# Offsets of weight units inside their SBUF places, by kind of product

## The chip, the cores and the metric

The kernel runs on one core of a Trainium2 chip. The metric is the device time of one execution in microseconds; the median of several runs is compared. Five engines work side by side: TensorE (PE) multiplies, and loads the stationary operand of a product with an instruction of its own (PEld) that overlaps the product before it; VectorE (DVE), ScalarE (ACT) and GpSimd (POOL) do elementwise work; SyncE (SP) issues most transfers.

## The reference

Two decoder layers over 1024 tokens of width 1024. Each layer forms a modulated RMS norm of its input, one wide projection, three mixers on parts of its columns (sliding-window attention, retention, gated linear attention), a gate on each, an output projection, and a gated residual:

```python
h = rms_norm(x, pre_gain) * (1.0 + scale) + shift
proj = h @ w_in                      # 1024 x 3088
(aq, ak, av, ag, rq, rk, rv, rg, gq, gk, gv, gg, ga) = jnp.split(proj, IN_SPLITS, axis=-1)
...
y = jnp.concatenate([a_out, r_out, g_out], axis=-1) @ w_out
return x + gate * rms_norm(y, post_gain)
```

All of it is float32.

## The kernel before

**Products.** A float32 product is made of three products of a reduced float32 type: each operand is split into a high and a low part, and high x high, low x high and high x low are summed in PSUM (`PASSES`, `accum`). A projection of one 128-token tile by 256 columns is thus 3 x 8 = 24 matmuls. The weights of 256 columns are called a unit. There are four kinds of products with a unit:

- **plain** (`project`): the hidden state of one tile is the stationary operand, 128 columns; the unit is the moving one, 256 columns (272 for `gg`, which carries the 16 columns of the decay gate's low rank). Units `rg`, `rq`, `rk`, `rv`, `gv`, `kv` and `gg`.
- **turned** (`project_T`): 128 columns of the unit are stationary, the hidden state of two pairs of tiles is moving, 512 columns. Units `gqk`, `aq0`, `aq1`, `ag0`, `ag1`.
- **out** (`y_half`, and `y_last` with 256 columns): in layer 0 a tile of the mixers' output, named `mx`, is stationary and two `o` units are moving.
- **block** (`prod`): layer 1's output uses a scheme with seven products of half-size weight blocks (`W00`, `T1` and so on). A block is moving, 512 columns; an `mx`, `ma` or `a22` tile is stationary. T4 of the last tile is done in halves of 256 columns.

**Places.** Units, hidden states and blocks live in seven places of two large tiles, arena0 (places 0 to 2) and arena1 (places 3 to 6); `PLACES` has tile, offset and row width of each, in elements of 4 bytes, and `place(i)` gives a place as [high or low, k, columns]. `PLACE` says which place a unit takes in each layer, `TOK` which places the four pairs of hidden states take, `SW` the blocks. A row (one k) of an ordinary place has 256 elements, 1024 bytes, so every row begins at the same address modulo 512. Places 0 and 2 are wide, for `gg`: a row has 288 elements, 1152 bytes, so successive rows begin 128 bytes later modulo 512. In layer 0 the units `gg`, `rk`, `gv`, `aq1`, `ag1` are in place 0 and one pair of hidden states, and later `o1`, in place 2; in layer 1 those five units are in place 2, and one pair in place 0. A block has rows of 512 elements, 2048 bytes.

**Addresses.** SBUF is filled pool by pool: constants, arena0, the work tiles, then arena1. arena0 begins at byte 19,456 of a partition, 38 x 512. The work pool follows it and begins with 11 small tiles of 64 bytes, so its larger tiles (`t1`, the tiles for `kT` and `ma`, `mx`, `t2`, the staging tiles with `a22`) begin at 192 modulo 512. arena1 begins, after a pad of `APAD` = 32 bytes, at 153,600, 300 x 512. `GPAD`, a pad at the head of the work pool, is 0. The constant identity is at 128 modulo 512. In all that follows the distance is that of the moving operand's start less the stationary's, modulo 512: 0 for plain and turned products (0, 128, 256, 384 in turn where one of the two is in a wide place), 320 for out and block products.

**Order.** TensorE's instructions run in an order written out by the program: `mult` and `transp` add to a clock, and `pump` puts in the steps of smaller jobs whose due time has come (decays, attention, retention, norms). That order does not depend on addresses. Weights come by `load`: a transfer into a staging tile, the split into high and low on ScalarE, VectorE and GpSimd (L154, L542, L550), a flag for the products that wait.

Of the kernel before, what the change touches and what calls it, by code (L numbers as in the profile page):

```python
# [23 lines left out]
KT = D // P  # L24
# [16 lines left out]

LOG_CLAMP = -24.0

SLOT = KT * 512
WIDE = KT * 576
PLACES = {0: (0, 0, 288), 1: (0, WIDE, 256), 2: (0, WIDE + SLOT, 288)}
PLACES.update({3 + i: (1, i * SLOT, 256) for i in range(4)})
PLAIN = 2
SW = dict(W00=6, T1=3, W11=4, W10=5, T2=2, T3=0, T4=1)
TOK = ((1, 2, 3, 4), (3, 4, 0, 1))  # L50
PLACE = []
# [40 lines left out]
def trunk(ctx: ExitStack, tc: tile.TileContext, ins, cst, out):  # L92
# [3 lines left out]
    def skew(pool, name, n):  # L96
        if n:
            pool.tile([P, n // 4], F32, name=name, tag=name, bufs=1)
# [39 lines left out]

    arenas = [bp.tile([P, 2 * WIDE + SLOT], F32R, name="arena0")]

    def place(i):
        n, o, w = PLACES[i]
        return arenas[n][:, o:o + 2 * KT * w].rearrange("p (a k n) -> p a k n", a=2, k=KT)

    def both(x, y):
# [324 lines left out]


    def unit(l, name):
        return place(PLACE[l][name])


    queue, flying = [], []
# [35 lines left out]
    def used(l, name):  # L512
        await_flag(("w", l, name))
        return unit(l, name)

    def load(l, name, first=None):
        if l >= DEPTH:
            return
        c0 = COLS[name]
        src = w_out[l] if name[0] == "o" else w_in[l]  # L520
        wt = unit(l, name)
        sv = src.rearrange("(k p) n -> p k n", p=P)

# [35 lines left out]


    def sw(name):
        n, o, _ = PLACES[SW[name]]
        return arenas[n][:, o:o + KT * 512].rearrange("p (a k n) -> p a k n", a=2, k=4)

    def sw_load(k, i, j):
# [5 lines left out]
    def sw_split(name, k, st, key):  # L571
        w = sw(name)
        copy("sh" + key, w[:, 0, k], st)
        eng("sl" + key).tensor_tensor(w[:, 1, k], st, f(w[:, 0, k]), ALU.subtract)
# [8 lines left out]
    def sw_first(name):  # L583
        def conv(k, x, y=None):
            if y is not None:
                sw_diff(x, 0, k, x, y)
            if name[0] == "W" and name[1] == "1" and k > 1:
                w, g = sw(name), gnc[:, DEPTH - 1:DEPTH]
                A.activation(w[:, 0, k], x, AF.Copy, scale=g)
                V.scalar_tensor_tensor(w[:, 1, k], x, g, f(w[:, 0, k]), ALU.mult, ALU.subtract)  # L590
            else:
                sw_split(name, k, x, f"w{k}")
            if k == 3:
                flag(("sw", name))

        for k in range(4):
            if name == "T1":
                request(DEPTH - 1, 2, lambda k=k: (sw_load(k, 0, 1), sw_load(k, 0, 0)), lambda *s, k=k: conv(k, *s))
            else:
                i, j = int(name[1]), int(name[2])  # L600
                request(DEPTH - 1, 1, lambda k=k: (sw_load(k, i, j),), lambda *s, k=k: conv(k, *s))
# [62 lines left out]
    def pre(l, t, xt, early=False, soon=False):  # L664

        p, tt = divmod(t, 2)
        if tt == 0:
            hT[(l, p)] = place(TOK[l][p])
# [94 lines left out]
    skew(ap, "apad", APAD)  # L763
    arenas.append(ap.tile([P, 4 * SLOT], F32R, name="arena1"))
    with tc.issue_after(mark[0].ins), tc.issue_after(mark[3].ins):
# [497 lines left out]
    def prod(dst, a, name, start=True, stop=True, c=slice(0, 512)):  # L1263

        w = sw(name)
        await_flag(("sw", name))
        q = 0
        for i, j in PASSES:
            for k in range(4):
                mult(dst, a[:, i, k, :], w[:, j, k, c], start and q == 0, stop and q == 11)  # L1270
                q += 1
        pump()
# [411 lines left out]
B2, B1, BS, BST, MMB, SMB = 10, 8, 11, 5, 3, 3  # L1684
EN = {"shw0": "V", "shw1": "A", "shw2": "A", "shw3": "A", "slw0": "V", "slw1": "G", "slw2": "V", "slw3": "G", "sht2": "A", "sht3": "A", "sht4": "A", "slt2": "V", "slt3": "G", "slt4": "G", "sd": "V", "mh0": "A", "mh1": "A", "mh2": "A", "mh3": "A", "mf": "A", "ms0": "V", "ms1": "V", "ms2": "V", "ms3": "V", "yg0": "V", "yg1": "V", "ml0": "V", "ml1": "V", "ml2": "V", "ml3": "V", "mod0": "A", "mod1": "V", "qst": "S", "smh": "S", "sml": "S", "sm0": "S", "sm1": "S", "lao": "S", "sao": "S", "lmix": "S", "ssg": "S", "lsg": "S", "ssr": "S", "lsr": "S", "lx": "S", "sx": "A", "lw": "S", "lwm": "S", "whi0": "V", "whi1": "A", "whi2": "A", "whi3": "A", "wlo0": "V", "wlo1": "V", "wlo2": "V", "wlo3": "G", "xn0": "V", "xn1": "V", "hlo0": "V", "hlo1": "V", "rot0": "V", "rot1": "V", "rdec": "V", "kslo": "V", "qslo": "V", "vlo": "G", "kT": "A", "qT": "A", "sprev": "A", "pn": "G", "pf0": "A", "aoc": "A", "hng": "V", "mh": "A", "gso": "V", "mg": "V", "mgl": "V", "rT": "A", "rv": "A", "gv": "A", "gk": "A", "ak0": "V", "ak1": "V", "ak2": "V", "ak3": "V", "kd0": "G", "kd1": "G", "kd2": "G", "kx1": "G", "kx2": "G", "kx3": "V", "kx4": "V", "qb": "G", "stx": "V"}
L = {"sw1": 0.4, "ld1": 1.2, "ld2": 1.2, "ld1@1": 1.2, "ld2@1": 1.27, "swW00": 0.0, "swT1": 0.0, "swW11": 0.4, "swW10": 0.5, "tt1": 8.0, "tt2": 1.75, "tb1": 24.5, "tb2": 0.75, "pf3": 13.2, "pf1": 6.35, "pf2": 4.16, "mod1": 4.6, "mod2": 4.0, "mod3": 13.29, "mod4": 7.04, "mod5": 3.36, "mod6": 9.04, "pre1": 7.44, "kv1": 3.1, "kv2": 2.11, "aq1": 6.0, "aq7": 6.0, "ag1": 5.44, "aq2": 2.4, "aq6": 5.2, "aq3": 10.21, "aq4": 7.36, "aq5": 3.6, "hn1": 8.93, "hn2": 2.85, "gz1": 11.18, "gz2": 8.13, "gl1": 2.76, "gd3": 15.9, "gc1": 0.62, "gc2": 1.94, "gc3": 1.33, "gc4": 0.87, "gc6": 0.86, "gc5": 1.14, "rc1": 0.8, "rc2": 1.09, "rc3": 5.87, "rc4": 2.51, "fin1": 7.28, "lay1": 1.13, "gc4@1": 0.93, "mod2@1": 4.0, "mod3@1": 15.1, "mod5@1": 3.36, "mod6@1": 4.11, "pre1@1": 7.44, "kv1@1": 2.79, "kv2@1": 5.28, "aq1@1": 4.8, "aq7@1": 5.28, "ag1@1": 6.25, "aq2@1": 0.82, "aq6@1": 6.0, "aq3@1": 10.9, "aq4@1": 4.4, "aq5@1": 5.15, "hn1@1": 8.12, "hn2@1": 2.85, "gz1@1": 15.91, "gz2@1": 10.94, "gl1@1": 4.6, "gd3@1": 15.9, "gc1@1": 0.48, "gc2@1": 1.94, "gc3@1": 1.33, "gc6@1": 0.86, "gc5@1": 1.04, "rc1@1": 0.37, "rc2@1": 0.84, "rc3@1": 1.9, "rc4@1": 2.79, "fin1@1": 4.28, "lay1@1": 1.7}
CPAD, GPAD, APAD = 0, 0, 32
CHUNK = 7
LAG = 2
VDB = 8  # L1690
# [32 lines left out]
```

## Time and profile before

| | |
|---|---|
| median of 3 runs | 1008.04 us (1007.93 to 1008.37) |
| the profiled execution | 1009.94 us |
| its span, first to last instruction | 1008.2 us |
| TensorE busy | 971.4 us, 7133 products |
| weight loads busy | 829.8 us |
| VectorE, ScalarE, GpSimd busy | 689.2, 411.5, 233.5 us |
| mean granted TensorE clock | 0.984 |

The page and the trace's other views come from that one profiled execution. A busy share is the part of the span in which an engine works on something; products are pipelined and overlap their neighbours, so the time that one product really takes in a run is read from the spacing of starts, not from its mean duration. The chain of work that ended last is followed back from the last instruction to what released it, and so on; time on it is time that the end waits for. In a line such as `L170 PE MATMUL mm<-arena,mx 128*128 128x256 f32 x48 | 5.6, 276 | 0.0`, L170 is the line of the kernel (in the helper `mult`), mm is the PSUM tile written, arena and mx the tiles read, 128x256 the moving operand, x48 the count; then busy time in us, the mean of one in ns, and the idle time before. "mm<-arena,arena" are products with one operand in each arena tile, "mm<-arena" those with both in the same.

Between 40 and 320 us lie layer 0's projections with their mixers, from 320 to 530 its query and gate products, attention and output; 530 to 800 and 800 to 908 are the same for layer 1, and from 908 on its output in blocks.

### The profile page before, as it was taken

To read this page: it belongs to the slowest core of one execution; us is meant where nothing else is said; L and a number is where in the kernel's file an instruction comes from. 1 tells how busy PE (TensorE), PEld (TensorE's weight loads), DVE (VectorE), ACT (ScalarE), POOL (GpSimd) and SP (SyncE) were. 2 spreads that over 40 slices of the span, in tenths; PEclk is the share of its full clock that TensorE was granted. 3 is DMA by queue.
4 is the path that set the end of the run, shared out by engine and by line. 5 is a ranking of instruction groups with operands and counts; after the bars stand their busy time and mean duration, and the time that the engine had idled before them with its cause. 6 is when DMAs were issued, how large, how long until landed. Compare 5 with 4: busy or idle time off the path is not lost.

```text
span 1008.2 us, 19624 instructions
## 1 busy us (share of the span) xinstructions
PE 971.4 (96%) x7133; PEld 829.8 (82%) x7133; DVE 689.2 (68%) x1698; ACT 411.5 (41%) x1152; POOL 233.5 (23%) x275
## 2 busy tenths in 40 slices
PE   5798999999999999999999999999999999999996
PEld 1498999978998777777889999997899877777775
DVE  3779856847766688664488295685676577676876
ACT  2466421323332556643355242123333266563321
POOL 2210101232420234430113010113232033544100
PEclk8899999999999999999999999999999999999999
DMA  9832612423325245668646151343132433388884
GB/s 307 298 98 74 194 48 86 140 92 117 114 85 178 89 137 157 206 185 266 212 148 210 53 167 44 104 132 109 47 111 85 126 89 122 115 246 253 262 258 140
DMA packets 129969, 148.77 MB, mean 148 GB/s; under 512 B 14113, under 2 KB 94285, under 8 KB 129873
## 3 DMA queue, kind: packets, MB, share of 16 engines
q1 hardware_dynamic: 124176, 137.96, 44.8%
q10 hardware_dynamic: 5696, 9.56, 2.6%
q8 instruction: 56, 0.92, 0.4%
q14 instruction: 41, 0.33, 0.1%
HBM read 109.20 MB, written 36.18 MB: 144 GB/s over the span
## 4 chain that ended last, share of the span: by engine, by line
PE 76%; DVE 9%; DMA 5%; issue 4%; POOL 2%; ACT 2%; ACTq 0%; POOLq 0%; SPq 0%; DVEq 0%
PE mm L170 58%; PE aux L170 14%; PE aux L185 4%; DMA st<-in_w_in_dram 2%; POOL sm L645 2%; DMA xk<-in_x_dram 1%; DVE arena L542 1%; DMA a<-mixS 1%; DVE arena L718 1%; DMA st<-in_w_mod_dram 0%; DMA st<-in_w_out_dram 0%; DVE t L1257 0%; DVE t L335 0%; DVE t L676 0%; DVE t L710 0%
## 5 line engine op out<-in xcount | busy, mean ns | idle before, releaser
L170 PE MATMUL mm<-arena 128*128 128x256 f32 (+2 forms) x1824 | 300.2, 318 | 4.3 <-DVE t L1003 2.5
L170 PE MATMUL mm<-arena,arena 128*128 128x256 f32 (+2 forms) x1824 | 301.3, 319 | 1.8 <-DVE t L1003 1.8
L170 PEld LDWEIGHTS mm<-arena 128*128 128x128 f32 x1824 | 255.5, 191 | 28.9 <-issue 3.3
L170 PEld LDWEIGHTS mm<-arena,arena 128*128 128x128 f32 x1824 | 255.4, 191 | 26.3 <-issue 5.8
L645 POOL TENSOR_TENSOR sm<-sm,mhalf 128x1 f32<-128x1 f32 (+1 forms) x64 | 56.3, 880 | 350.4 <-DVE sm L644 335.2
L170 PE MATMUL mm<-arena,mx 128*128 128x512 f32 (+1 forms) x564 | 131.2, 389 | 2.1 <-ACT kept L1350 2.0
L170 PEld LDWEIGHTS mm<-arena,mx 128*128 128x128 f32 x564 | 102.4, 190 | 26.1 <-ACT kept L1350 2.4
L154 ACT ACTIVATE t<-aux 128x256 f32<-128x256 f32 (+2 forms) x124 | 55.9, 468 | 74.1 <-PE aux L185 61.8
L154 ACT ACTIVATE arena<-st 128x512 fp32r<-128x512 f32 x94 | 56.0, 626 | 53.1 <-PE mm L170 19.3
L542 POOL TENSOR_TENSOR arena<-st,arena 128x512 fp32r<-128x512 f32 x31 | 43.8, 1415 | 135.4 <-ACT arena L154 97.7
L940 POOL TENSOR_TENSOR smx<-smx,sm 128x512 f32<-128x512 f32 x32 | 35.7, 1117 | 127.2 <-DVE sm L939 119.8
L542 DVE TENSOR_TENSOR arena<-st,arena 128x512 fp32r<-128x512 f32 x77 | 59.5, 793 | 5.1 <-ACT arena L154 2.9
L936 ACT ACTIVATE smx<-smx,sm 128x129 f32<-128x129 f32 x128 | 49.9, 392 | 29.5 <-DVE sm L933 29.5
L185 PE MATMUL aux<-c_ident,t 128*128 128x128 f32 (+1 forms) x292 | 48.6, 284 | 7.9 <-DVE t L676 7.7
L372 DVE SCALAR_TENSOR_TENSOR acc<-st,c_act,acc 128x512 f32<-128x512 f32 x60 | 46.1, 768 | 13.0 <-DMA st<-in_w_mod_dram 12.5
L185 PEld LDWEIGHTS aux<-c_ident,t 128*128 128x128 f32 (+1 forms) x292 | 35.4, 145 | 14.9 <-DVE t L676 9.5
L170 PEld LDWEIGHTS aux<-t,mx 32*128 32x128 f32 (+1 forms) x896 | 39.5, 187 | 3.9 <-issue 2.2
L984 ACT ACTIVATE t<-aux 128x256 f32<-128x256 f32 x32 | 12.3, 384 | 73.6 <-PE aux L170 64.3
L708 ACT ACTIVATE t<-aux,mod,mod 128x128 f32<-128x128 f32 x68 | 25.8, 461 | 37.0 <-DVE t L1257 18.6
L170 PE MATMUL aux<-t,mx 32*128 32x32 f32 (+1 forms) x896 | 40.6, 272 | 0.0
L931 DVE COPY_PREDICATED smx<-c_curmask,aux 128x256 f32<-128x256 int32 x64 | 25.4, 445 | 18.3 <-ACT smx L154 14.8
L1257 DVE SCALAR_TENSOR_TENSOR t<-t,sm,t 128x512 f32<-128x512 f32 x32 | 24.0, 780 | 19.0 <-DMA t<-in_x_dram 11.2
(223 smaller groups left out, 1380.6 us busy)
## 6 DMA issues: line engine op xcount, KB each, us to landing
st<-in_w_in_dram SPq DMA_DIRECT2D x96, 256.0 KB, 3.1
st<-in_w_mod_dram SPq DMA_DIRECT2D x64, 256.0 KB, 2.8
st<-in_w_out_dram SPq DMA_DIRECT2D x52, 256.0 KB, 4.5
mx<-mixS SPq DMA_DIRECT2D x20, 512.0 KB, 5.1
mixS<-t SPq DMA_DIRECT2D x72, 128.0 KB, 3.6
wm<-in_w_mod_dram SPq DMA_DIRECT2D x12, 512.0 KB, 6.4
t<-in_x_dram SPq DMA_DIRECT2D x24, 256.0 KB, 4.4
t<-tabS SPq DMA_DIRECT2D x16, 256.0 KB, 4.1
```

The source lines that it names most:

```text
L154: A.activation(dst, src, AF.Copy)
L170: T.matmul(dst, lhsT, rhs, start=start, stop=stop)
L185: T.transpose(dst, src, idn)
L372: V.scalar_tensor_tensor(acc, wt, c_act[:, k:k + 1], acc, ALU.mult, ALU.add)
L542: e.tensor_tensor(lo, st, f(hi), ALU.subtract)
L645: G.tensor_tensor(r, r, mhalf[:, :w], ALU.pow)
L708: A.activation(hf[:, ks], at[kt], AF.Identity, scale=gain, bias=shift)
L931: V.copy_predicated(sv, curmask.unsqueeze(1).to_broadcast((P, 2, P)), pv[:, :, n // P - 1, :])
L936: A.activation(sm[:, h, :], sm[:, h, :], AF.Exp, bias=mx[:, h:h + 1], accum_out=sums[:, h:h + 1])
L940: eng("pn").tensor_tensor(sm[:, :, 0:128], sm[:, :, 0:128], rs.unsqueeze(2).to_broadcast((P, 4, P)), ALU.mult)
L984: A.activation(sq, po, AF.Square)
L1257: V.scalar_tensor_tensor(xt[j], yg[j], r, xt[j], ALU.mult, ALU.add)
```

## The change

The row width leaves `PLACES` and is given by whoever asks for a place: 256 elements for all but `gg`, which gets 320 (1280 bytes, so that its rows begin 0 and 256 bytes further modulo 512 in turn). No row of another unit or hidden state is 1152 bytes wide any more. Places grow by 128 elements, and a unit begins some elements into its place: 80 elements (320 bytes) for plain units and `gg`, 0 for turned and `o` units, 64 elements (256 bytes) for blocks. Hidden states begin at 0. `GPAD` becomes 320 bytes, which moves all work tiles by 320 (the larger ones then begin at 0 modulo 512), and `APAD` 224, so that with both pads arena1 is moved by 512 bytes and by the growth of arena0, which is a multiple of 512.

The distances after it are 320 for plain products (320 and 64 in turn for `gg`), 0 for turned, 0 for out and 256 for block products. What is computed, the number and order of TensorE's instructions and all transfers stay.

```diff
-SLOT = KT * 512
-WIDE = KT * 576
-PLACES = {0: (0, 0, 288), 1: (0, WIDE, 256), 2: (0, WIDE + SLOT, 288)}
-PLACES.update({3 + i: (1, i * SLOT, 256) for i in range(4)})
+SLOT = KT * 512 + 128
+WIDE = KT * 640 + 128
+PLACES = {0: (0, 0), 1: (0, WIDE), 2: (0, WIDE + SLOT)}
+PLACES.update({3 + i: (1, i * SLOT) for i in range(4)})
+TURNED = ("gqk", "aq0", "aq1", "ag0", "ag1")
+PLAIN_AT, TURNED_AT, OUT_AT, BLOCK_AT = 80, 0, 0, 64
...
-    def place(i):
-        n, o, w = PLACES[i]
+    def place(i, at=0, w=256):
+        n, o = PLACES[i]
+        o += at
         return arenas[n][:, o:o + 2 * KT * w].rearrange("p (a k n) -> p a k n", a=2, k=KT)
...
     def unit(l, name):
-        return place(PLACE[l][name])
+        at = OUT_AT if name[0] == "o" else TURNED_AT if name in TURNED else PLAIN_AT
+        return place(PLACE[l][name], at, 320 if name == "gg" else 256)
...
     def sw(name):
-        n, o, _ = PLACES[SW[name]]
+        n, o = PLACES[SW[name]]
+        o += BLOCK_AT
         return arenas[n][:, o:o + KT * 512].rearrange("p (a k n) -> p a k n", a=2, k=4)
...
-CPAD, GPAD, APAD = 0, 0, 32
+CPAD, GPAD, APAD = 0, 320, 224
```

## The prediction

> **What bounds the kernel now.** I read the busy shares first, then the chain of work that ended last, then that chain stage by stage, and last the spacing of single runs of products. All but the last two views are on the page or the answer about stages.
>
> ```profile
> span 1008.2 us, 19624 instructions
> PE 971.4 (96%) x7133; PEld 829.8 (82%) x7133; DVE 689.2 (68%) x1698; ACT 411.5 (41%) x1152; POOL 233.5 (23%) x275
> PE 76%; DVE 9%; DMA 5%; issue 4%; POOL 2%; ACT 2%; ACTq 0%; POOLq 0%; SPq 0%; DVEq 0%
> ```
>
> TensorE is busy for 96% of the span and makes up 76% of the chain. The other 24% are stretches in which it waits for a chain through VectorE, a transfer or GpSimd, and there a faster product gains nothing. The change touches only products of 128 rows that write a tile called mm (and a few that write aux), so I need their share of the path by stage. The first view has the busy time of all instructions that touch mm (its first PE number); the lines after it are the chain's shares in the same five stretches, in the same order.
>
> ```profile
> 40.00:320.00 280.00, 214.91 (x1480) 195.07 (x1481) 26.89 (x98) 18.41 (x56) 0.98 0.37 113
> 320.00:530.00 210.00, 171.25 (x699) 128.01 (x698) 24.21 (x36) 14.24 (x36) 1.00 0.56 176
> 530.00:800.00 270.00, 219.21 (x1562) 200.68 (x1561) 29.49 (x103) 20.15 (x62) 1.00 0.36 107
> 800.00:908.00 108.00, 76.01 (x297) 53.21 (x296) 11.86 (x18) 4.09 (x7) 1.00 0.47 142
> 908.00:1009.00 101.00, 68.95 (x296) 54.53 (x295) 13.14 (x20) 3.49 (x6) 0.96 0.71 226
> ...
> by line: PE mm L170 47.2%; PE aux L170 13.3%; issue 6.2%; PE aux L185 3.6%; POOL sm L645 3.0%; DMA st<-in_w_in_dram 2.7%; DVE arena L718 1.9%; DMA st<-in_w_mod_dram 1.8%; DVE arena L542 1.4%; DVE t L710 1.4%; DVE t L676 1.1%; DMA mixS<-t 1.
> by line: PE mm L170 78.8%; PE aux L170 15.3%; PE aux L185 6.0%
> by line: PE mm L170 61.9%; PE aux L170 13.4%; PE aux L185 4.0%; DMA st<-in_w_in_dram 3.5%; issue 3.0%; POOL sm L645 2.3%; DVE arena L542 1.5%; DVE t L1257 0.8%; DVE mx L1105 0.8%; POOL mx L802 0.7%; DVE t L990 0.6%; DVE t L1096 0.5%; DVE mx
> by line: PE mm L170 67.6%; PE aux L170 25.6%; PE aux L185 7.2%
> by line: PE mm L170 43.7%; DMA a<-mixS 7.8%; PE aux L170 6.4%; DMA st<-in_w_out_dram 4.9%; issue 4.3%; DMA t<-xs 3.2%; DVE t L1359 2.9%; DVE t L1354 2.8%; DVE t L1257 2.7%; POOL arena L574 2.7%; ACT st L1358 1.6%; DVE st L609 1.3%; DVE mx L
> ```
>
> Dividing path time by busy time gives the share of these products that counts: 0.472 x 280 / 214.9 = 0.61 in 40 to 320 us (layer 0's projections), 0.788 x 210 / 171.3 = 0.97 in 320 to 530 (its query and gate products and its output), 0.619 x 270 / 219.2 = 0.76 in 530 to 800 (layer 1's projections), 0.96 in 800 to 908 and 0.64 in the last stretch.
>
> How many products of each kind there are, from the groups kept apart by shape (name, shape, count, busy time, mean of one):
>
> ```profile
> L170 PE MATMUL mm<-arena,arena 128*128 128x256 f32 x1152 | 151.8, 286 | 0.0
> L170 PE MATMUL mm<-arena 128*128 128x256 f32 x1152 | 151.3, 286 | 2.5 <-DVE t L1003 2.5
> L170 PE MATMUL mm<-arena,mx 128*128 128x512 f32 x516 | 125.7, 400 | 2.1 <-ACT kept L1350 2.0
> L170 PE MATMUL mm<-arena,arena 128*128 128x512 f32 x480 | 123.3, 405 | 0.0
> L170 PE MATMUL mm<-arena 128*128 128x512 f32 x480 | 121.1, 400 | 0.0
> L170 PE MATMUL mm<-arena,mx 128*128 128x256 f32 x48 | 5.6, 276 | 0.0
> L170 PE MATMUL mm<-arena,a 128*128 128x256 f32 x24 | 3.0, 280 | 0.0
> ```
>
> So 2304 plain products of 256 columns, 960 turned ones of 512 columns; the gate unit gg adds 384 of 272 columns.
>
> **The change part by part.** No instruction is added, removed or put in another order; no transfer or wait is added. Only addresses move. What does the distance cost today? The timeline of TensorE has runs of one kind (start, length, count); the last three lines are pieces of the chain in order of time, in the same form. A run's spacing is the start of what follows less its own start, over its count, or its length less one mean duration, over count minus one.
>
> ```profile
> 530.46 5.84 PE L170 MATMUL mm<-arena,mx 128*128 128x512 f32 x49
> 536.14 7.91 PE L170 MATMUL mm<-arena,arena 128*128 128x272 f32 x62
> ...
> 586.16 5.92 PE L170 MATMUL mm<-arena 128*128 128x256 f32 x48
> 591.92 3.00 PE L170 MATMUL mm<-arena,arena 128*128 128x256 f32 x24
> 594.76 0.27 PE L185 MATMUL aux<-c_ident,ga 128*48 128x128 f32 x1
> ...
> 997.36 2.99 PE L170 MATMUL mm<-arena,a 128*128 128x256 f32 x24
> ...
> 334.71 2.66 PE L170 MATMUL mm<-arena 128*128 128x512 f32 x11
> ...
> 313.79 16.61 PE mm L170 x72
> 468.80 12.02 PE mm L170 x52
> 972.51 13.74 PE mm L170 x60
> ```
>
> Distance 0: the 48 products from 586.16 have weights and hidden state in plain 1,024-byte rows of arena 1, so moving minus stationary is 0 mod 512 throughout: (591.92 - 586.16) / 48 = 120.0 ns. With one operand in a wide place (1,152-byte rows; distance walks 0, 128, 256, 384), the 24 from 591.92 take (594.76 - 591.92) / 24 = 118.3 ns. Distance 320 is there already: layer 0's y_last multiplies o units, at 0, with an mx tile, at 192, and (192 + 320) is 512. Its run from 530.46 is one product of 512 columns, about 0.23 us by the rows below, and 48 of 256: (5.68 - 0.23) / 48 = 113.5 ns. The weight loads show it too:
>
> ```profile
> L170 PEld LDWEIGHTS mm<-arena 128*128 128x128 f32 x48 | 5.8, 192 | 0.0
> L170 PEld LDWEIGHTS mm<-arena,mx 128*128 128x128 f32 x47 | 5.4, 188 | 0.0
> ```
>
> One load takes 192 ns in the run at distance 0 and 188 ns in y_last's. That speaks for a meeting of the two reads. It isn't the whole story: the half-wide products of T4 at 997.36 are at 320 too, and take (2.99 - 0.28) / 23 = 117.8 ns. T4's rows are 2,048 bytes apart, y_last's moving rows 1,024 as the plain units' are, so y_last is the nearer row, and I take 113.5 with 117.8 as the other end.
>
> *Plain, 2304 products, to 320.* Of six plain units per layer two (rk, gv) lie in a wide place, and one of four hidden-state pairs does, so half the products (4/6 x 3/4) are at a constant 0 and save 6.5 ns; the others save 118.3 - 113.5 = 4.8. Mean 5.6, of which I count 93%, as the first one or two of 24 start after other work: 5.2 ns. 1152 in each projection stretch: 6.0 us of TensorE time each; on the path 0.61 x 6.0 + 0.76 x 6.0 = 8.2 us.
>
> *gg, 384 products.* Its run at 536.14 has (7.91 - 0.29) / 61 = 124.9 ns, with 0.29 for the last one's own duration. After, its 1,280-byte rows alternate between 320 and 64. No row shows 64; bounds are the present 125 and, with 256-column excess kept, 113.5 x 272/256 = 120.6. Midway, 2.3 ns: 0.9 us on TensorE, 0.6 on the path.
>
> *Turned, 960 products, to a clean 0.* The 72 at 313.79 (partly wide) have 16.61 / 72 = 230.7 ns. The 11 at 334.71 lie wholly in arena 1 at distance 0 and take (2.66 - 0.39) / 10 = 227.0. What is gained is that no unit or hidden state is strided any more: 3.7 ns, 87% of them in undisturbed runs, 3.1 us on TensorE, 2.8 on the path (most lies in the stretches with 0.96 and 0.97).
>
> *Layer 0's output, 360 products of 512 columns, from 320 to 0.* The 52 at 468.80 have 12.02 / 52 = 231.2 ns; at the turned run's 227.0, 4.2 ns, 1.5 us. y_last's 48 go from 113.5 to 120.0, plus 0.3 us of TensorE. There GpSimd's clearing of a gla tile is on the chain, not TensorE (a piece of the chain, quoted here), so it costs nothing; with that cover gone, 0.3.
>
> ```profile
> 530.92 1.82 POOL mx L802
> ```
>
> *Blocks of layer 1's output, some 330 products, from 320 to 256.* No run is at a constant 256. Now 13.74 / 60 = 229.0 ns. Bounds: 222.5 (the whole 6.5 ns between 120.0 and 113.5 gained) and 236 (the slowest spacing of a longer run: (337.75 - 331.14) / 28, quoted below). I take no change, as the rows at 320 and at a clean 0 lie only 2 ns apart; the ends are -1.4 and +1.5 us at 0.64.
>
> ```profile
> 331.14 6.68 PE L170 MATMUL mm<-arena 128*128 128x512 f32 x28
> 337.75 0.98 PE L170 MATMUL aux<-kT,mx 64*128 64x256 f32 x12
> ```
>
> *Side effects.* GPAD moves every work tile by 320. Products between two work tiles keep their distance. Transposes read the constant identity against a work tile, so theirs changes from 448 to 128. No row has 128; they hold about 4% of the chain (L185 in the lines above), 42 us, and if they spread by the same 6% as 113.5 to 120 do, that is 2.5 us either way; I take 0. Both arenas stay at a multiple of 512 (320 + 192 more bytes before arena 1).
>
> Sum: 8.2 + 0.6 + 2.8 + 1.5 = 13.1 us. VectorE, next with 9% of the chain, may be late in places where TensorE now ends it; I take 13. The profiled execution took 1009.94 us, 1.7 beyond its span and 1.9 above the median of 1008.04; it would be 997, and a median run **995.0 us**.
>
> The page "SBUF — State Buffer" of the Trainium skill, section "Who interferes with whom", speaks against all this: TensorE's two read ports (moving operand and weight load) are independent, and TensorE never waits on anyone in SBUF. By that rule addresses cost nothing and the sum would be 0. The trace of this case disagrees at 120.0 against 113.5 ns for one shape, but agrees in so far as 117.8 comes close to 118.3.
>
> **The rivals.**
> - *320 is worth little (T4's row).* y_last's 113.5 is then due to its stationary tile (rows of 512 bytes), and plain products settle near 117.8: 2.2 ns where they were at 0, 0.5 on the others, mean 1.35 x 0.93 x 2304 = 2.9 us, 2.0 on the path; with the other terms (0.6 of gg halved) 6.6: 1001.5 us. For it: 24 products at 320. Against it: 48 products, nearer in row step. 20%.
> - *Address is not the cause.* The spread comes from neighbours (other engines' traffic, entry into the run); the change does not do what it says: 1008 us. For it: one distance has both 113.5 and 117.8. (The page of the Trainium skill named above would make this the outcome.) Against it: the run of 48 at distance 0 holds 120.0 with a slower weight load throughout. 10%.
> - *Slower: 320 is the worse place for a full sweep.* The hidden state as stationary, in 1,024-byte rows, meets the moving read at 320 in the middle of each sweep, as 512-column products show it: 229.0 at 320 against 227.0 at 0. Plain products then cost 2 ns or more above 120; at 124, near gg's present spacing, +4.9 ns on 2304 x 0.69 = 7.8 us, less the 4.3 of turned and output: 1011.5 us, or 1013 with blocks at their upper end. It decides from about 121.6 ns for plain. 7%.
> - *Another engine becomes the bound.* In the stretches with 0.61 and 0.76 the weight conversions on VectorE and the transfers of w_in are already on the chain; if they are late wherever plain runs get short, two thirds of the 8.2 go: 1000.5 us. 9%.
>
> **How the numbers follow.** The forecast, 995.0, has 54%; its own range is 989 to 1000 (blocks -1.4 to +1.5, transposes 2.5 either way, gg, and up to 3 us hidden). With 20, 10, 7 and 9% for the rivals the range for 8 in 10 is 988 to 1004: it leaves out the no-change and slower cases. Faster by over 0.2% (about what a measurement tells from no change, 2 us): 54 + 20 + 9 = 83%; same 10%; slower 7%.
>
> **What would show it.** Right: plain runs of 48 near 113 to 114 ns with weight loads of 188 ns, runs of turned products with 227 and less spread, TensorE busy down by 15 to 18 us, the gain found in 40 to 320 and 530 to 800. Wrong: plain runs at 117 or above, blocks above 230, or TensorE's busy time down without the span following, with w_in transfers and VectorE growing on the chain.

## The result and the profile after

| | before | changed |
|---|---|---|
| median of 20 runs each, us | 1008.14 | 1004.82 |
| lowest and highest, us | 1004.78, 1011.52 | 1001.55, 1007.72 |
| profiled execution, us | 1009.94 | 1001.56 |

The ratio is 0.9962 (95% interval 0.995 to 0.9974): 3.8 us less, 2.6 to 5.0 (the medians differ by 3.3). The forecast was 995.0, with 988 to 1004 as range; the direction was right, the forecast gain more than three times too large. The two profiled executions differ by 8.4 us, more than twice what the medians say, as single runs of one kernel spread over 6 to 7 us. What the change did is therefore read from spacings.

The page of the changed kernel (span, busy shares, chain by engine):

```profile
span 999.8 us, 19626 instructions
PE 964.1 (96%) x7133; PEld 827.7 (83%) x7133; DVE 691.6 (69%) x1698; ACT 410.8 (41%) x1152; POOL 235.2 (24%) x275
PE 75%; DVE 10%; DMA 7%; issue 3%; ACT 3%; POOL 1%; SPq 0%; POOLq 0%; DVEq 0%; ACTq 0%
```

The bound is where it was: TensorE 96% busy and three quarters of the chain. Part of the 8.4 us lies even ahead of the products that were changed. The piece of the chain with the first four products that read the modulation's weights ends at 26.87 us in before and at 25.05 in the changed kernel: 1.8 us of the difference arise before any unit is used. In e6, the changed kernel executed again (below), the same piece ends at 26.59. That is run-to-run spread and no gain of the change.

Now the timeline of TensorE in the changed kernel, at the places that were shown of before (start, length, count):

```profile
523.20 6.37 PE L173 MATMUL mm<-arena,mx 128*128 128x512 f32 x50
529.41 8.02 PE L173 MATMUL mm<-arena,arena 128*128 128x272 f32 x62
...
579.12 5.82 PE L173 MATMUL mm<-arena 128*128 128x256 f32 x48
584.77 2.99 PE L173 MATMUL mm<-arena,arena 128*128 128x256 f32 x24
...
308.43 7.53 PE L173 MATMUL mm<-arena,arena 128*128 128x512 f32 x32
315.79 9.23 PE L173 MATMUL mm<-arena 128*128 128x512 f32 x40
324.95 0.77 PE L173 MATMUL aux<-kT,mx 64*128 64x128 f32 x10
...
964.10 5.60 PE L173 MATMUL mm<-arena,mx 128*128 128x512 f32 x24
969.54 2.88 PE L173 MATMUL mm<-arena,a 128*128 128x512 f32 x12
...
988.58 3.03 PE L173 MATMUL mm<-arena,a 128*128 128x256 f32 x24
```

Read as before. The 48 plain products at 579.12, now at distance 320, take (584.77 - 579.12) / 48 = 117.7 ns; before, at 0, it was 120.0. That is not y_last's 113.5 but the 117.8 of T4's halves. y_last itself, moved from 320 to 0, takes (529.41 - 523.20 - 2 x 0.23) / 48 = 119.8, where it had 113.5. T4's halves, moved from 320 to 256, take (3.03 - 0.28) / 23 = 119.6. gg takes (8.02 - 0.29) / 61 = 126.7, where it had 124.9: worse. The 72 turned products at 308.43 have (324.95 - 308.43) / 72 = 229.4, where they had 230.7, and the blocks from 964.10 on (969.54 - 964.10) / 24 = 226.7, where they had 229.0. The weight loads tell distances 320 and 0 apart (the plain run, then y_last; the second number behind the first bar is the mean duration in ns):

```profile
L173 PEld LDWEIGHTS mm<-arena 128*128 128x128 f32 x47 | 5.6, 188 | 0.0
...
L173 PEld LDWEIGHTS mm<-arena,mx 128*128 128x128 f32 x47 | 5.7, 192 | 0.0
```

The two kinds have changed roles: with 256 columns 192 ns belongs to distance 0, not to a kind of product. y_last shows one thing more. Its moving o units begin at 0 in both kernels; only mx, the stationary operand, was moved, and the spacing went from 113.5 to 119.8. So the moving operand's own address doesn't set the price by itself.

So that all kinds can be compared over all kernels, this table has the mean spacing from one product's start to the next one's, in ns, over all products of a kind, without those that were followed by other work or a wait (spacings of over 136, 143 and 243 ns for 256, 272 and 512 columns are left out, and with them most first products of a run after other work; 86 to 97% of a kind remain). It is worked out from the single records of each kernel's trace; the kernels' labels are explained below.

```
                     plain   gg     turned  output 512  blocks 512
before               118.9   124.6  231.2   231.3       229.0
changed              117.7   126.5  229.1   227.9       227.3
e2_plain0            119.7   125.5  229.2   227.9       227.5
e3_plain384          118.7   126.5  229.2   227.9       227.4
e5_plain32_gg448     117.1   123.9  229.1   227.9       227.3
e7_worst             119.7   125.4  234.0   234.2       234.2
e8_plain112          115.3   125.1  229.1   227.9       227.4
e9_plain192          115.8   123.5  229.1   227.9       227.4
e10_plain112_gg192   115.4   123.5  229.2   227.8       227.2
products, about      2160    340    830     344         320
```

The output's 231.3 before mixes two things. Half of these products read o1, which lay in a wide place: the 15 runs of 24 fall into eight at 232.3 to 233.3 ns and seven at 229.0 to 230.2, as many as there are with o1 and without. After, the same two groups have 227.7 and 228.0 on the mean. So by the move from 320 to 0 alone a product gains 1.5 ns, and by that and the end of the stride together 5.2; the prediction's "from 320 to 0" at 231.2 took the mixture for the distance.

### The profile page after: what moved, and what is told of

The parts are those of the page before. It is cut to its first block, busy times and chain, and to the rows that moved or that the text cites. A ratio compares the mean times of both kernels' runs of the same rounds, so it can differ in the third digit from the quotient of the medians.

```text
span 999.8 us, 19626 instructions
## 1 busy us (share of the span) xinstructions
PE 964.1 (96%) x7133; PEld 827.7 (83%) x7133; DVE 691.6 (69%) x1698; ACT 410.8 (41%) x1152; POOL 235.2 (24%) x275
## 4 chain that ended last, share of the span: by engine, by line
PE 75%; DVE 10%; DMA 7%; issue 3%; ACT 3%; POOL 1%; SPq 0%; POOLq 0%; DVEq 0%; ACTq 0%
PE mm L173 57%; PE aux L173 14%; PE aux L188 4%; DMA st<-in_w_in_dram 2%; POOL sm L650 1%; DMA st<-in_w_out_dram 1%; DVE arena L546 1%; DMA wm<-in_w_mod_dram 1%; DMA t<-mixF 1%; DMA xk<-in_x_dram 1%; DVE arena L723 1%; DMA mx<-mixS 1%; DVE t L715 1%; DMA st<-in_w_mod_dram 0%; DVE t L338 0%
## 5 line engine op out<-in xcount | busy, mean ns | idle before, releaser
L173 PE MATMUL mm<-arena,arena 128*128 128x256 f32 (+2 forms) x1824 | 297.7, 316 | 0.3 <-DVE t L1008 0.3
L173 PEld LDWEIGHTS mm<-arena,arena 128*128 128x128 f32 x1824 | 252.5, 188 | 23.7 <-issue 4.1
L173 PE MATMUL mm<-arena,mx 128*128 128x512 f32 (+1 forms) x564 | 128.3, 384 | 1.7 <-ACT kept L1355 1.7
```

The costliest lines, as they stand in the source:

```text
L173: T.matmul(dst, lhsT, rhs, start=start, stop=stop)
```

## The experiments

The theory after the result: the distance sets a few steady spacings, and 320 has two of them, 113.3 and 117.8. Rival A: y_last's 113.5 came from its stationary tile, whose rows are 512 bytes apart where a hidden state's are 1024. Rival B: the address is not the cause at all.

**e1_map: the price by itself.** A kernel with nothing but products. Each run of 24 has the three passes of `accum`; only the moving operand's offset changes.

```diff
+DIST = [int(d) for d in range(0, 512, 32)]
...
+                s0 = STAT + (a * KT + k) * sstep
+                m0 = MOV + d // 4 + (w * KT + k) * mstep
...
+    for d in DIST:
+        for m in (4, 2, 1):
+            turns(m)
+            run("wide", d)
+        for m in (4, 5, 6):
+            turns()
+            run("fill", 320, m, 512)
+            run("wide", d)
```

> Only products are run, on the input's values, and nothing of the layers is computed: per distance 0 to 480 in steps of 32 bytes, runs of 24 products of 256 columns (rows of 1024 bytes; six runs, entered from transposes or from products of 512 columns), of 256 columns with stationary rows of 512 bytes (two runs), of 272 columns with moving rows of 1280 bytes (two), of 512 columns in two halves (two). Theory 1 (the distance sets a small number of steady spacings, and 320 has two of them): at 320 most runs settle at 117.8 ns and a few at 113.3, whatever the stationary row; at 0 and 256 all at 120.0; near 116.7 at 384; 512 columns 226.7 at 0 and 256 and 229 at 320; 272 columns 126.7 at 320. Rival A (the stationary tile's rows of 512 bytes made the 113.5 of the kernel before): the runs with 512-byte stationary rows give 113.3 at 320 and those with 1024-byte rows 117.8. Rival B (address is not the cause): one spacing at all distances.

Mean spacing of a run's last products, ns; where the runs of a distance differ, the lowest and highest. Distances from 256 on repeat the value 256 below to 0.1 ns (wide at 160 and 416: 118.6 and 118.5 highest), so one period is given.

```
distance                  0/256  32/288  64/320  96/352  128/384      160/416      192/448      224/480
256, rows of 1024 (6x)    120.0  116.7   117.8   120.0   118.4-120.0  117.1-118.6  113.3-117.8  118.1-118.5
256, stat. rows 512 (2x)  120.0  116.7   117.8   120.0   118.2-120.0  117.2-118.6  113.3-117.8  118.3-118.5
272, rows of 1280 (2x)    125.6  125.8   126.7   125.4-  126.7        123.3-123.8  123.3        125.4-126.7
                                                 126.7
512 in two halves (2x)    226.7  233.3   228.9   233.3   232.9        234.3        233.3        233.3
```

Three runs of 256 columns in the timeline, at distances 0, 320 and 448, each seen through a window that leaves out a run's beginning (the row's start is that of its first product in the window):

```profile
39.32 2.08 PE L57 MATMUL wide<-arena 128*128 128x256 f32 x16
...
530.15 2.16 PE L57 MATMUL wide<-arena 128*128 128x256 f32 x17
...
722.81 1.86 PE L57 MATMUL wide<-arena 128*128 128x256 f32 x15
```

(2.08 - 0.28) / 15 = 120.0 ns, (2.16 - 0.28) / 16 = 117.5 and (1.86 - 0.28) / 14 = 112.9, each to some 0.7 by the rows' rounding. The core ran nothing else, so rival B falls. Rival A falls too: stationary rows of 512 and of 1024 bytes give the same spacings. e1 moves the moving operand alone; that the stationary one counts as much is shown by y_last above and by e7 below, whose turned units, stationary, are moved to distance 160 and take 234.0 where the map has 234.3. The theory holds, with two corrections: the period is 256 bytes, not 512, so 320 is the same place as 64, and in this quiet kernel 320 gave 117.8 in eight runs of eight; the two states appeared at 192 and 448 (113.3 once, 117.8 five times, at equal distances and with only the run ahead of them differing). At 384 the 116.7 that was expected did not come.

**e2_plain0 and e3_plain384: plain units elsewhere in the changed kernel.**

```diff
-PLAIN_AT, TURNED_AT, OUT_AT, BLOCK_AT = 80, 0, 0, 64
+PLAIN_AT, TURNED_AT, OUT_AT, BLOCK_AT = 0, 0, 0, 64
```

That is e2; e3 has 96 elements for plain.

> The changed kernel with plain units and gg at 0 instead of 320 bytes, all else as changed: what is left is the gain of turned, output and block products and of the unstrided rows. Theory 1: plain runs at 120.0 ns, 2.2 ns above the changed kernel, about 2300 x 0.93 x 2.2 = 4.7 us more TensorE time, two thirds of it on the path, so 3 us slower than the changed kernel and within 1.5 us of before (ratio to before 0.998 to 1.001). Rival B: the same time as the changed kernel (0.996).

> The changed kernel with plain units and gg at 384 bytes instead of 320. Theory 1, with the rows of the kernel before at a constant 384 (116.7 ns for 256 columns, 123.3 for 272): plain runs 1.1 ns and gg 3.4 ns below the changed kernel, 2.4 + 1.2 us of TensorE time, two thirds on the path: 2.4 us faster than the changed kernel, ratio to before about 0.994. Rival B: the same time as the changed kernel.

e2: 0.9988 of before (0.9968 to 1.0008), median 1007.58. Plain runs of 119.7 ns in the table, 2.0 above the changed kernel's. The ratio lies in the 0.998 to 1.001 expected, 2.6 us above the changed kernel's 0.9962, where the table gives (2.0 x 2160 - 1.0 x 340) x 0.69 = 2.7 (0.69 is the prediction's path share of plain products, the mean of 0.61 and 0.76). The two intervals overlap (the changed kernel's is 0.995 to 0.9974), so the times alone hardly tell them apart; the spacings do. It isn't the plain units' share in the gain over before either, as 119.7 is itself dearer than before's 118.9. Whether turned and output alone gain anything isn't shown by the time, only by their spacings. e3: 0.9977 (0.996 to 0.9994), and not the 0.994 expected. Plain takes 118.7 ns and gg 126.5, as the map has them at 384. The 116.7 of before "at a constant 384" had been read where unit and hidden state both lie in wide places. Both begin at 0 there and their rows step together, so the distance is 0 throughout and not 384; e4 gives 116.7 for such rows at 0.

**e4_finer: steps of 8 bytes, and rows that step.** The same kernel with `range(0, 256, 8)`, and runs whose moving rows (or both operands' rows) are 1088 or 1152 bytes apart.

> Again products alone, nothing of the layers: distances 0 to 248 in steps of 8 bytes (the first map repeats after 256), 256 columns entered in three ways, 272 columns (rows of 1280 bytes), 512 columns; and at every 32 bytes 256 columns whose moving rows, or both operands' rows, step by 1088 or 1152 bytes. Theory 1: the spacings move between 113 and 120 ns (256 columns) and 226 and 235 (512) in steps of 64 bytes or less, the two-state places lie around 192, and none lies steadily below 116.7. Rival (a line of 32 bytes or more is what counts): the eight distances within 32 bytes give the same spacing.

```
256 columns, three entries each, ns (the middle one where they differ by less than 0.6)
distance   0      8      16           24     32           40     48     56     64     104    112          120
spacing    120.0  120.0  113.3-118.7  120.2  116.7-117.8  120.0  118.3  120.0  117.8  120.0  113.3-114.8  122.2
distance   128          136          144          168    176    184    192    200          208    232    248
spacing    118.4-120.0  120.4-121.2  118.2-119.1  122.3  119.3  120.0  113.3  120.0-122.2  118.9  123.0  121.3
512 columns: 226.7 at 0, 246.7 at 104, 238.8 at 72, 240.0 at 88 and 168, 228.8 at 64; the other distances 231 to 240
both operands' rows 1152 bytes apart: 116.7 at seven of eight distances, 120.0 at 224; both 1088: 117.3 to 120.0
moving rows alone 1088 or 1152 bytes apart: 116.7 to 118.8
```

These are means over a run's last twelve products. Eight bytes decide: 112 has 113.3 (114.8 from one entry, which comes to 113.4 in its last eight) between 120.0 at 104 and 122.2 at 120. The rival, that all distances within 32 bytes cost the same, falls, and so does my "none lies steadily below 116.7": 112 and, here, 192 do. No odd multiple of 8 is below 119.7.

**e5_plain32_gg448 and e6_after_again.**

```diff
-PLAIN_AT, TURNED_AT, OUT_AT, BLOCK_AT = 80, 0, 0, 64
+PLAIN_AT, TURNED_AT, OUT_AT, BLOCK_AT = 8, 0, 0, 64
+GATE_AT = 112
...
-        return place(PLACE[l][name], at, 320 if name == "gg" else 256)
+        at, w = (GATE_AT, 320) if name == "gg" else (at, 256)
+        return place(PLACE[l][name], at, w)
```

> The changed kernel with plain units at 32 bytes (116.7 ns in the first map) and gg at 448 (rows then at 448 and 192, 123.3 ns). Theory 1: plain runs 1.1 ns and gg 3.4 ns below the changed kernel, 2.4 + 1.2 us of TensorE time, two thirds on the path: 2.4 us faster than the changed kernel, ratio to before 0.994. Rival (the path no longer takes gains in the projection stretches): the same as the changed kernel.

> The changed kernel beside the others on one chip: ratio to before 0.995 to 0.9975, by all theories.

e5: 0.9957 (0.9938 to 0.9976), median 1003.47; the changed kernel beside it: 0.997 (0.9948 to 0.9991), median 1004.75. Plain is at 117.1 and gg at 123.9, so the map carries over, but 1.3 us between the medians, where 2.4 were expected and the table gives (0.6 x 2160 + 2.6 x 340) x 0.69 = 1.5, lies within the intervals: the time decides neither for the theory nor for the rival.

**e7_worst: the dear distances.**

```diff
-PLAIN_AT, TURNED_AT, OUT_AT, BLOCK_AT = 80, 0, 0, 64
+PLAIN_AT, TURNED_AT, OUT_AT, BLOCK_AT = 0, 24, 40, 40
```

> The changed kernel with plain units and gg at 0 (distance 0, 120.0 ns), turned units at 96 bytes (distance 160, 234.3), o units and blocks at 160 bytes (distance 160, 234.3). Theory 1, by the first map: turned 7.6 ns x 830 x 0.93 = 5.9 us, output 2.5, blocks 1.6, plain 3.3: 13 us slower than the changed kernel, ratio to before about 1.009. If the address is not the cause, or the path hides it: within 3 us of the changed kernel.

1.0061 (1.0039 to 1.0084), median 1014.11: 0.0099 above the changed kernel's ratio, 10 us where 13 were expected (9.4 by the medians against e6, which ran beside it). Distances alone make 1% between two kernels. The 13 took the map's steady spacings (234.3 against 226.7). By the table the kinds differ by 4.9 ns (turned), 6.3 (output), 6.9 (blocks) and 2.0 (plain), gg gaining 1.1; with the counts in its last line and the path shares of the prediction (0.93, 0.97, 0.64, 0.69, 0.69) that is 3.8 + 2.1 + 1.4 + 3.0 - 0.3 = 10.0 us. The path shares thus agree with the time, within its interval of some 3 us; what was off is that turned products at the beginning of a run aren't at the steady spacing (229.1 on the mean, 226.7 at the end).

**e8_plain112, e9_plain192, e10_plain112_gg192: the state that the forecast had counted on.**

```diff
-PLAIN_AT, TURNED_AT, OUT_AT, BLOCK_AT = 80, 0, 0, 64
+PLAIN_AT, TURNED_AT, OUT_AT, BLOCK_AT = 28, 0, 0, 64
```

That is e8; e9 has 48 elements for plain, and e10 has 28 and, as e5, a `GATE_AT`, here of 48.

> The changed kernel with plain units and gg at 112 bytes. In the finer map 256 columns took 113.3 to 114.8 ns there from all three entries, and 272 columns 123.3. Theory 1, and with it the forecast's own sum at a price of 113.5: plain runs 4.4 ns and gg 3.3 ns below the changed kernel, 2160 x 4.4 = 9.5 and 1.1 us of TensorE time, two thirds on the path: 7 us faster than the changed kernel, about 0.990 of before. Rival (a quiet map doesn't carry over; with the layers' other work the runs fall into the slower state): plain at 117 to 120, within 2 us of the changed kernel.

> The changed kernel with plain units and gg at 192 bytes. The two maps had 113.3 ns in four of nine runs there and 117.8 in five; 272 columns 123.3. Theory 1: between the changed kernel and the one at 112 bytes, 1 to 6 us faster than the changed kernel, with plain runs at one of the two spacings and little in between. Rival: plain at 117.8 throughout, gg alone faster, 0.7 us.

> The changed kernel with plain units at 112 bytes and gg at 192 (rows at 192 and 448). Theory 1: plain runs at 113.3 ns as with 112 before, gg at 123.4 throughout: 0.5 us faster than with both at 112, ratio to before 0.989 to 0.993, some 5 us faster than the changed kernel. Rival (the projection stretches are full of other waits by now): no faster than 0.9925.

e8: 0.9917 (0.9888 to 0.9946), median 1000.62. e9: 0.9909 (0.9879 to 0.994), 999.80. e10: 0.9909 (0.9881 to 0.9936), 999.53. All three are faster than both kernels, by 8 to 9 us against before and some 5 against the change; between the three the times don't decide. The timeline of e8:

```profile
572.94 4.92 PE L173 MATMUL mm<-arena,arena 128*128 128x256 f32 x41
577.71 5.60 PE L173 MATMUL mm<-arena 128*128 128x256 f32 x48
```

and of e9, the same stretch:

```profile
569.60 5.08 PE L173 MATMUL mm<-arena,arena 128*128 128x256 f32 x41
574.51 5.82 PE L173 MATMUL mm<-arena 128*128 128x256 f32 x48
```

The 48 from 577.71 take (5.60 - 0.28) / 47 = 113.2 ns in e8, and in e9 (5.82 - 0.28) / 47 = 117.9: the larger of the two spacings, at a distance that gave 113.3 elsewhere in the same trace (of its 48 runs of 20 products or more, 30 end at 113.3 and 18 at 117.8). The rival in e9's expectation, 117.8 throughout, falls. The 41 in front, which follow other work, take (577.71 - 572.94) / 41 = 116.3 in e8 and (574.51 - 569.60) / 41 = 119.8 in e9: a run loses some 90 ns on its first product (203 ns to the next start for 113), and in e8 the next five take 116 to 121 ns before 113.3 is reached. That is no exception in e8: without the spacings that the table leaves out, the first ten products of a run have 117.4 ns on the mean and the later ones 113.5, and 1105 of the 2304 plain products are among the first ten of theirs. So e8 gets 115.3, not 113.3; its gg, with 125.1, misses the map's 123.3 too. Its expected 7 us over the changed kernel became (0.9962 - 0.9917) x 1008 = 4.5; by the table (2.4 x 2160 + 1.4 x 340) x 0.69 = 3.9. With an interval of 2.9 us to either side the time alone doesn't exclude the 7; the spacings do. e9 and e10 came out in their expected ranges; e10's interval takes in its rival's 0.9925.

## Why the prediction was wrong

With the table's spacings and counts and the prediction's own path shares, the sum can be made again, term by term (us on the path):

| term | predicted | measured | |
|---|---|---|---|
| plain, to 320 | 8.2 | 1.8 | (118.9 - 117.7) x 2160 x 0.69 |
| gg | 0.6 | -0.4 | (124.6 - 126.5) x 340 x 0.69 |
| turned, unstrided | 2.8 | 1.6 | (231.2 - 229.1) x 830 x 0.93 |
| layer 0's output, to 0 | 1.5 | 1.1 | (231.3 - 227.9) x 344 x 0.97 |
| blocks, to 256 | 0 | 0.3 | (229.0 - 227.3) x 320 x 0.64 |
| sum | 13.1 | 4.4 | time: 3.8 (2.6 to 5.0) |

**The step that failed is the price of a plain product at 320: 113.5 ns in the prediction, 117.7 measured.** That alone is 4.2 x 2160 x 0.69 = 6.3 of the 8.7 us by which the sum was too high, and it is the prediction's own sign of being wrong, plain runs at 117 or above. The prediction had two rows at that distance, 113.5 and 117.8, and took the first because "y_last is the nearer row" in row steps. Stationary rows of 512 or 1024 bytes make no difference (e1); moving rows of 2048 bytes, as T4's, weren't run by themselves, but 117.8 is also what rows of 1024 take at 320. Both prices are states of the same distance. Of the changed kernel's 48 plain runs of 20 products or more one, from 103.9 us, is at 113.3 and 47 at 117.8, and in e6, the same kernel again, this run is at 117.8 as well (the changed kernel, then e6):

```profile
103.90 2.98 PE L173 MATMUL mm<-arena,arena 128*128 128x256 f32 x24
106.72 0.27 PE L188 MATMUL aux<-c_ident,ga 128*48 128x128 f32 x1
```

```profile
105.47 3.07 PE L173 MATMUL mm<-arena,arena 128*128 128x256 f32 x24
108.38 0.27 PE L188 MATMUL aux<-c_ident,ga 128*48 128x128 f32 x1
```

With 0.20 us for the first product, the other 23 take (106.72 - 103.90 - 0.20) / 23 = 113.9 ns and (108.38 - 105.47 - 0.20) / 23 = 117.8: same program, same addresses, another spacing. What puts a run at one or the other, and y_last at 113.3, stays open. The rival that 320 is worth little had the price right and 20%, but not the reason (y_last's stationary rows), and its time, 1001.5, held the other terms too high.

**The second part of the same term is settling.** The forecast counted 93% of the products at the steady spacing. At 112, where e8 does reach 113.3, the mean is 115.3, and the term comes to (118.9 - 115.3) x 2160 x 0.69 = 5.4 us, not 8.2. Whether runs at 320 that come to 113.3 would settle as slowly isn't shown; the one that did had 113 ns from its second product on. Turned products settle slowly too: 226.7 at the end of a run and 229.1 on the mean, which is most of why their term came to 1.6 us instead of 2.8.

**gg had the wrong sign.** It was put midway to a bound carried over from y_last. The map's 64 and 320 are one place for its rows, and it costs 126.7 where some 122.6 had been taken. The row of before (distances 0 and 128 in turn) was the better one.

**What held.** The mechanism: the distance sets the spacing. The weight load's duration is no measure of it, though: 192 ns goes with distance 0 and 256 columns, but 188 stands beside 113.3, beside 117.8 and, at 96 in e1, beside 120.0. That turned and output gain by a clean 0 (226.7 at the end of a run, 227.0 forecast). That y_last loses 6.5 ns per product; but that it costs nothing behind GpSimd's clearing didn't hold: in the changed kernel's profiled execution a piece of the chain of 72 products, from 522.90 to 532.11 us, takes in all of y_last's 48, so the 0.3 us that the prediction gave for that case count, and the sum of 4.4 becomes 4.1. What also held are the path shares: with them the sums come out at 4.4 or 4.1 for 3.8 here, 10.0 for 10 in e7 and 3.9 for 4.5 in e8, each within the time's interval. So the gain was not lost on the way to the end of the kernel; it wasn't made on TensorE. Transposes, at 128 instead of 448 from the identity, were put at nothing and are: they follow each other at 109.3 ns before and 109.1 after, 0.1 us over all 432.

The rule of the Trainium skill, page "SBUF — State Buffer", section "Who interferes with whom" (independent ports, TensorE waits on nobody), is not borne out: in e1, with no other work, one shape takes 113.3 to 120.0 ns by the offset of one operand alone. What inside the memory makes the two reads meet isn't shown by any run here.

## What to carry to other kernels

Where weight loads and products overlap back to back, the offset between the two operands is worth 1% and more of a kernel like this one (1.0061 of before in e7, 0.9909 in e9), and it can be measured in one run of bare products over all offsets; two rows of a trace that disagree at one offset call for that measurement rather than for a choice. Price a steady spacing over whole runs, beginnings included: in e8 the mean lay 2 ns above it. An offset at which nearly every run ends at 113.3, but some only after ten products (112), and one at which runs are there sooner, but 18 of 48 stay at 117.8 (192), come to nearly the same mean, 115.3 and 115.8.

## What was not expected of the hardware

- The spacing repeats after 256 bytes, and steps of 8 bytes change it: 256 columns 113.3 to 123 ns, 512 columns 226.7 (0) to 246.7 (104).
- One offset can have two steady states, 113.3 and 117.8 ns, and a run of 48 products stays in the one that it fell into (e9).
- 512 columns are best at 0, where 256 columns are at the top of what multiples of 32 bytes take (120.0).
